# Weight tiles padded to whole multiples of 512 bytes in a one-core decoder block

## The chip, the cores and the metric

The kernel runs on one core of a Trainium2 chip. The metric is the device time of one execution in microseconds. Three executions of the kernel before took 2819.47, 2820.7 and 2825.2 us; the median is 2820.7.

## The reference

One layer of a hybrid decoder block on x (512 tokens, 2048 channels), in float32:

```
mod = silu(c) @ w_ada + b_ada                  # six rows of 2048: shift, scale, gate, twice
h   = rmsnorm(x, norm_mix_g) * (1 + sc_m) + sh_m
a_b, a_c, a_x, q, f_logit, i_in, g_out, gate_a, gate_b = split(h @ w_in)   # 2048 -> 11264
y_a = (a_b * causal_depthwise_conv(a_c * a_x)) @ w_conv_out
y_b = (rmsnorm(hgrn2_chunked(silu(q), 1 - f, i_in, log f)) * silu(g_out)) @ w_hgrn_out
x   = x + gt_m * ((sigmoid(gate_a) * y_a + sigmoid(gate_b) * y_b) @ w_o)
h2  = rmsnorm(x, norm_ffn_g) * (1 + sc_f) + sh_f
x   = x + gt_f * ((silu(h2 @ w_ffn_gate) * (h2 @ w_ffn_up)) @ w_ffn_down)  # 2048 -> 5632 -> 2048
out = rmsnorm(x, norm_final_g)
```

## The kernel before

Activations lie transposed, channels on partitions, 512 tokens along the row. Every large product is made in split precision: weights and activations are each cut into a rounded part (hi) and the remainder (lo), both of type float32r, and each product becomes three matmuls, hi on hi, hi on lo and lo on hi. `mm3` (L228) issues them on L233, L234 and L235 for the projections; `m3` (L628) on L629, L630 and L631 for the gates and the FFN. The weights are the operand that is loaded into the array, 128 x 128 at a time; the activations stream past, 512 or 256 columns of them. `v_block` (L344) is the exception: there the activations are loaded and the weight tile streams, 256 columns at a time.

A weight tile comes in by a DMA on SP's queue as a raw tile (`w_dma`, `g_dma`, `u_dma`), ScalarE casts it to hi, VectorE subtracts hi from it to make lo (L166 and L167 in `w_prep`; `quad_s` at L673 for Strassen quads; L1085 and L1086 in `u_prep` otherwise). The hi and lo tiles are made by `w_tile` (L138) from pools with three buffers of each, `wp` (L84, up to the output projection) and `wp2` (L1050, the FFN), and one of 16 for the tail (`us["pool"]`, L1235). The buffers of a pool come round in the order first, third, second.

The stages, in order of time: the first projections together with the norm and the first adaLN rows; the remaining projections (`proj`, 512 columns streaming) with the HGRN core and the convolution as background work on VectorE, interleaved by step counts; the gates (`st_pass`, 256 columns: one level of Strassen's scheme, seven products on a quad of 128 x 128 blocks); the branch outputs and the output projection, with the other 128 tiles of `w_ada` reduced on VectorE meanwhile (`mods`, L593; two buffers `wm`); the FFN, whose gate and up passes are Strassen passes of 256 columns, and whose `down` (L1159) has 512 columns; the tail, 256 columns.

Where the tiles lie: `w_tile` makes a tile of a*b + 32 elements of 4 bytes and starts the weights at its first element, or, when `half` is set, at the 17th (`WOFF` = 16 elements, 64 bytes). `half` is set for weights past which 256 columns stream. A tile of 1024 weights is 4224 bytes, 8 x 512 + 128; one of 896 is 3712 bytes, 7 x 512 + 128. So consecutive buffers drift by 128 bytes modulo 512. In `wp` the hi buffers start at bytes 117760, 121984 and 126208 of a partition (0, 128 and 256 modulo 512), the lo buffers at 130432, 134656 and 138880 (384, 0 and 128). In `wp2` they start at 39936, 43648 and 47360 (0, 128, 256) and 51072, 54784 and 58496 (384, 0, 128). With the order of the buffers, successive weight tiles have hi/lo at 0/384, 256/128 and 128/0 when 512 columns stream, and at 64/448, 320/192 and 192/64 when 256 do. Activations lie at 0 (`h`, `o`, `sa`, `sx`) or, behind `wp2`, at 256 (`hc`, `sb`). Eight weight pairs of the FFN's first up pass are kept inside `sb` tiles for its second half (kind H of `u_prep`), at 256, with 256 columns streaming.

Of the kernel before, what the change touches and what calls it, by code (L numbers as in the profile page):

```python
# [9 lines left out]
F32R = mybir.dt.float32r  # L10
# [4 lines left out]
P = 128  # L15
# [29 lines left out]
WOFF = 16  # L45
# [17 lines left out]
def hybrid_block_kernel(ctx: ExitStack, tc: tile.TileContext, xt, cols, crow, wam, war, wst, win, wco, who, wo, wgt, wg, wu, wd,  # L63
# [4 lines left out]
    def nm(s):  # L68
        cnt[0] += 1
        return f"{s}{cnt[0]}"  # L70
# [62 lines left out]
        return t.rearrange("p a b -> p (a b)")  # L133

    wlist = []
    wstate = {"dma": 0, "prep": 0, "use": 0, "raw": {}, "hl": {}, "half": ()}

    def w_tile(pool, shape, tag, name, half):  # L138
        a, b = shape[1:]
        t = pool.tile([P, a * b + 32], F32R, tag=tag, name=nm(name))  # L140
        o = WOFF if half else 0
        return t[:, o:o + a * b].rearrange("p (a b) -> p a b", b=b)

    def w_pair(shape, half=False):
        return [w_tile(wp, shape, t, t, half) for t in ("hi", "lo")]
# [824 lines left out]
    torder = [(j, 0) for j in range(TU)] + [(j, 1) for j in range(TU)] + [(j, u) for j in range(TU, 8) for u in range(2)]  # L970
    ulist.extend((wd[j, 10], u, "D" if i < TU else "T") for i, (j, u) in enumerate(torder))
    kept = []
    us = {"dma": 0, "prep": 0, "use": 0, "raw": {}, "hl": {}, "pool": None, "after": ()}

    def u_dma():
        i = us["dma"]
# [86 lines left out]
    def u_prep():  # L1063
        i = us["prep"]
        while i not in us["raw"]:
            u_dma()
        _, u, kind = ulist[i]
        raw = us["raw"].pop(i)[:, u, :, :]
        pool = us["pool"] if kind == "T" else wp2
        shp = [P, 4, P] if kind == "T" else [P, 7, P]  # L1070
        if kind == "H":
            k = len(kept)
            t = sb[k // 2][k % 2]
            hi, lo = (t[:, 1 + 2 * b:3 + 2 * b, :].rearrange("p a (c n) -> p (a c) n", n=P) for b in range(2))
            kept.append((hi, lo))
        else:
            hi = w_tile(pool, shp, "hi", "uh", kind != "D")
            lo = w_tile(pool, shp, "lo", "ul", kind != "D")
        if kind == "S":
            quad_s(wp2.tile([P, 4, P], F32, tag="sm", name=nm("us"), bufs=2), raw, hi, lo)  # L1080
        else:
            with ExitStack() as order:
                for ins in us["after"] if i >= len(ulist) - 12 else ():
                    order.enter_context(tc.issue_after(ins.ins))
                S.copy(hi[:, 0:4, :], raw)  # L1085
                V.tensor_tensor(lo[:, 0:4, :], raw, hi[:, 0:4, :].bitcast(F32), op=ALU.subtract)  # L1086
        us["hl"][i] = (hi, lo)
        us["prep"] = i + 1
# [315 lines left out]
```

## Time and profile before

| | |
|---|---|
| median of three runs | 2820.7 us |
| the profiled execution | 2818.55 us |
| its span, first to last instruction | 2816.8 us |
| TensorE matmul busy | 2741.5 us (97%), 18524 matmuls |
| TensorE weight loads busy | 2461.4 us (87%) |
| VectorE busy | 2217.8 us (79%) |
| ScalarE busy | 1100.1 us (39%) |
| mean granted TensorE clock | 0.991 |

How to read what follows. In a group's line stand the source line, the engine, the operation, the tile written and the tiles read (buffer numbers left out), the shapes, the count, and behind a bar the busy time in us and the mean duration of one instruction in ns, then the idle time before the group. Matmuls are pipelined: one's recorded duration runs on while the next has begun, so durations of successive matmuls overlap. What a matmul costs in a stream is the distance from its start to the next start. In the timeline a row begins with the start and the duration in us. A line of stretches gives its length and the busy time (and count) of TensorE's matmuls, its weight loads, VectorE, ScalarE and GpSimd, then the granted clock, the busy share of the DMA engines and GB/s. The chain is the work that ended last, followed back from the end of the stretch, by engine and line. Residues below are byte addresses modulo 512 within a partition.

### The profile page before, as it was taken

To read this page: it belongs to the slowest core of one execution; us is meant where nothing else is said; L and a number is where in the kernel's file an instruction comes from. 1 tells how busy PE (TensorE), PEld (TensorE's weight loads), DVE (VectorE), ACT (ScalarE), POOL (GpSimd) and SP (SyncE) were. 2 spreads that over 40 slices of the span, in tenths; PEclk is the share of its full clock that TensorE was granted. 3 is DMA by queue.
4 is the path that set the end of the run, shared out by engine and by line. 5 is a ranking of instruction groups with operands and counts; after the bars stand their busy time and mean duration, and the time that the engine had idled before them with its cause. 6 is when DMAs were issued, how large, how long until landed. Compare 5 with 4: busy or idle time off the path is not lost.

```text
span 2816.8 us, 46688 instructions
## 1 busy us (share of the span) xinstructions
PE 2741.5 (97%) x18524; PEld 2461.4 (87%) x18524; DVE 2217.8 (79%) x4326; ACT 1100.1 (39%) x1723; POOL 1.3 (0%) x7
## 2 busy tenths in 40 slices
PE   5999999999999999899999999999999999999997
PEld 3788888888799997787899899998989989898997
DVE  7998963836799996786789787796968879687786
ACT  4333422323245552222375343343434334343445
POOL 0000000000000000000000000000000000000000
PEclk8999999999999999999999999999999999999999
DMA  9865632322233348898744333333333333333333
GB/s 351 302 215 187 207 100 83 97 91 90 76 101 118 124 148 298 294 315 287 239 143 127 100 112 101 109 106 98 113 99 112 99 104 113 98 113 98 105 106 105
DMA packets 117616, 414.23 MB, mean 147 GB/s; under 512 B 12818, under 2 KB 17170, under 8 KB 117396
## 3 DMA queue, kind: packets, MB, share of 16 engines
q1 hardware_dynamic: 116244, 407.04, 43.9%
q10 hardware_dynamic: 1152, 4.19, 0.4%
q8 instruction: 145, 2.38, 0.4%
q14 instruction: 75, 0.61, 0.1%
HBM read 398.59 MB, written 12.59 MB: 146 GB/s over the span
## 4 chain that ended last, share of the span: by engine, by line
PE 81%; DVE 8%; DMA 8%; issue 2%; ACT 1%; SPq 0%; DVEq 0%; ACTq 0%
PE st L631 18%; PE st L630 18%; PE st L629 18%; PE m L233 7%; PE m L235 7%; PE m L234 7%; DMA wm<-in_war_dram 6%; DVE o L311 2%; DVE wm L311 1%; DVE lo L167 1%; PE x L488 1%; PE m L353 1%; PE m L351 1%; PE m L352 1%; PE m L631 1%
## 5 line engine op out<-in xcount | busy, mean ns | idle before, releaser
L233 PE MATMUL m<-h,hi 128*128 128x512 f32 (+1 forms) x1152 | 436.0, 380 | 18.2 <-ACT hi L166 14.8
L631 PE MATMUL st<-sb,ul 128*128 128x256 f32 x1638 | 452.4, 276 | 0.3 <-DVE ul L680 0.3
L630 PE MATMUL st<-sb,uh 128*128 128x256 f32 x1638 | 452.3, 276 | 0.0
L629 PE MATMUL st<-sb,uh 128*128 128x256 f32 x1638 | 452.2, 276 | 0.0
L235 PE MATMUL m<-h,lo 128*128 128x512 f32 (+1 forms) x1152 | 437.0, 379 | 7.9 <-DVE lo L167 7.7
L234 PE MATMUL m<-h,hi 128*128 128x512 f32 (+1 forms) x1152 | 435.1, 378 | 0.3 <-DVE h L338 0.3
L166 ACT CAST hi<-wr 128x1024 fp32r<-128x1024 f32 (+2 forms) x199 | 201.7, 1017 | 532.9 <-PE m L234 381.7
L167 DVE TENSOR_TENSOR lo<-wr,hi 128x1024 fp32r<-128x1024 f32 (+2 forms) x199 | 234.8, 1182 | 118.1 <-ACT hi L166 116.9
L674 ACT CAST uh<-ur 128x384 fp32r<-128x384 f32 x326 | 167.3, 513 | 362.0 <-PE st L630 239.5
L631 PEld LDWEIGHTS st<-sb,ul 128*128 128x128 f32 x1638 | 307.6, 188 | 1.0 <-DVE ul L680 0.5
L629 PEld LDWEIGHTS st<-sb,uh 128*128 128x128 f32 x1638 | 307.5, 188 | 0.4
L630 PEld LDWEIGHTS st<-sb,uh 128*128 128x128 f32 x1638 | 307.5, 188 | 0.0
L233 PEld LDWEIGHTS m<-h,hi 128*128 128x128 f32 x1152 | 219.7, 191 | 62.5 <-ACT hi L166 15.9
L235 PEld LDWEIGHTS m<-h,lo 128*128 128x128 f32 x1152 | 217.6, 189 | 52.8 <-DVE lo L167 13.2
L629 PE MATMUL st<-hc,uh 128*128 128x512 f32 (+1 forms) x656 | 256.9, 392 | 2.9 <-ACT hc L1245 2.0
L631 PE MATMUL st<-hc,ul 128*128 128x512 f32 (+1 forms) x656 | 257.5, 395 | 0.0
L630 PE MATMUL st<-hc,uh 128*128 128x512 f32 x648 | 255.4, 394 | 0.0
L234 PEld LDWEIGHTS m<-h,hi 128*128 128x128 f32 x1152 | 218.0, 189 | 42.7 <-DVE h L338 1.1
L1086 DVE TENSOR_TENSOR ul<-ur,uh 128x512 fp32r<-128x512 f32 x210 | 143.2, 686 | 141.0 <-ACT uh L1085 140.9
L1085 ACT CAST uh<-ur 128x512 fp32r<-128x512 f32 x210 | 129.0, 620 | 314.0 <-PE st L630 294.2
L680 DVE TENSOR_TENSOR ul<-us,uh 128x512 fp32r<-128x512 f32 x326 | 223.0, 684 | 1.7 <-ACT uh L678 1.6
L678 ACT CAST uh<-us 128x512 fp32r<-128x512 f32 x326 | 201.5, 618 | 51.1 <-DVE us L677 50.3
(306 smaller groups left out, 6199.0 us busy)
## 6 DMA issues: line engine op xcount, KB each, us to landing
wm<-in_war_dram SPq DMA_DIRECT2D x128, 512.0 KB, 4.5
wr<-in_win_dram SPq DMA_DIRECT2D x107, 512.0 KB, 3.5
ur<-in_wg_dram SPq DMA_DIRECT2D x96, 512.0 KB, 3.5
ur<-in_wu_dram SPq DMA_DIRECT2D x88, 512.0 KB, 3.5
ur<-in_wd_dram SPq DMA_DIRECT2D x88, 512.0 KB, 3.5
o<-in_wam_dram SPq DMA_DIRECT2D x64, 512.0 KB, 6.5
wr<-in_wgt_dram SPq DMA_DIRECT2D x60, 512.0 KB, 3.6
wr<-in_wo_dram SPq DMA_DIRECT2D x44, 512.0 KB, 4.2
```

The lines of the kernel that those rows point to most:

```text
L166: S.copy(flat(hi)[:, 0:nw], raw[:, 0:nw])
L167: V.tensor_tensor(flat(lo)[:, 0:nw], raw[:, 0:nw], flat(hi)[:, 0:nw].bitcast(F32), op=ALU.subtract)
L233: TE.matmul(ps, wh, ah, start=first, stop=False)
L234: TE.matmul(ps, wh, al, start=False, stop=False)
L235: TE.matmul(ps, wl, ah, start=False, stop=last)
L629: TE.matmul(ps, wh, ah, start=first, stop=False, skip_group_check=True)
L630: TE.matmul(ps, wh, al, start=False, stop=False, skip_group_check=True)
L631: return TE.matmul(ps, wl, ah, start=False, stop=last, skip_group_check=True)
L674: S.copy(hi[:, 0:3, :], raw[:, 1:4, :])
L678: S.copy(hi[:, 3:7, :], sm)
L680: V.tensor_tensor(lo[:, 3:7, :], sm, hi[:, 3:7, :].bitcast(F32), op=ALU.subtract)
L1086: V.tensor_tensor(lo[:, 0:4, :], raw, hi[:, 0:4, :].bitcast(F32), op=ALU.subtract)
```

## The change

`w_tile` makes its tiles larger. Outside the tail a tile has a*b + 16 elements rounded up to a multiple of 128 elements, which is 512 bytes: 4608 bytes for 1024 weights and 4096 for 896. The weights start at the first element or, with `half`, at the 17th, as before. So in `wp` and `wp2` all hi and lo weights with 512 columns lie at 0 modulo 512, and those with 256 columns at 64. In the tail's pool a tile keeps its 32 extra elements. `us` is made earlier, so that `w_tile` can tell the tail's pool. Six buffers grow by 384 bytes each, so whatever is allocated behind `wp` or `wp2` on the same side (`hc`, `sb`, the work tiles `b`, the tail's tiles) moves by 2304 bytes, 256 modulo 512.

```diff
+    us = {"pool": None}
...
     def w_tile(pool, shape, tag, name, half):
         a, b = shape[1:]
-        t = pool.tile([P, a * b + 32], F32R, tag=tag, name=nm(name))
         o = WOFF if half else 0
+        t = pool.tile([P, a * b + 2 * WOFF if pool is us["pool"] else (a * b + WOFF + 127) // 128 * 128], F32R, tag=tag, name=nm(name))
         return t[:, o:o + a * b].rearrange("p (a b) -> p a b", b=b)
...
-    us = {"dma": 0, "prep": 0, "use": 0, "raw": {}, "hl": {}, "pool": None, "after": ()}
+    us.update({"dma": 0, "prep": 0, "use": 0, "raw": {}, "hl": {}, "pool": None, "after": ()})
```

## The prediction

> **What bounds the kernel now.** I read the page's head first, then the chain that ended last, cut into stretches of the span, then the matmul groups, then single weight tiles.
>
> ```profile
> span 2816.8 us, 46688 instructions
> PE 2741.5 (97%) x18524; PEld 2461.4 (87%) x18524; DVE 2217.8 (79%) x4326; ACT 1100.1 (39%) x1723; POOL 1.3 (0%) x7
> ```
>
> TensorE is busy for 97% of the span. But a busy engine isn't everywhere the one that sets the end, so here is the chain cut into stretches. From 0 to 165 us:
>
> ```profile
> by line: DVE o L311 26.6%; DVE lo L167 9.9%; PE m L235 8.4%; PE m L233 7.6%; PE m L234 7.2%; issue 5.8%; DMA x<-in_xt_dram 5.4%; DVE x L335 3.5%; DVE h L338 3.4%; DVE b L360 2.8%; ACT hi L166 2.6%; SPq L291 1.9%; PE m L353 1.6%; ACT b L358
> ```
>
> From 165 to 780 us:
>
> ```profile
> by line: PE m L233 25.8%; PE m L235 25.4%; PE m L234 25.3%; PE x L488 4.9%; PE m L353 4.0%; PE m L352 4.0%; PE m L351 4.0%; PE x L545 1.2%; PE x L555 1.1%; PE x L535 0.9%; PE x L547 0.9%; issue 0.8%; PE x L516 0.7%; PE x L529 0.4%; ACT L743
> ```
>
> From 1063 to 1370 us:
>
> ```profile
> by line: DMA wm<-in_war_dram 53.9%; DVE wm L311 12.4%; issue 10.9%; DMA modrow<-c_scratch 7.7%; DVE lo L167 4.6%; DMA b<-u_scratch 1.7%; DVE o L218 1.6%; DVE x L905 1.5%; DVE b L904 1.5%; DVE x L890 1.1%; DVE x L914 0.9%; SPq L153 0.8%; DVE
> ```
>
> From 1525 to 2755 us:
>
> ```profile
> by line: PE st L631 33.1%; PE st L630 33.1%; PE st L629 33.0%; DMA ur<-in_wu_dram 0.4%; DVE x L914 0.1%; DVE ul L1086 0.1%; DVE us L675 0.1%; DVE hc L1244 0.1%; DVE hc L1251 0.1%; DVE hc L1254 0.0%; ACT e L1250 0.0%; DVE hc L1253 0.0%; DVE
> ```
>
> Stretch two (the projections, 165 to 780) and stretch four (the FFN, 1525 to 2755) are TensorE almost alone: a nanosecond off a matmul there is a nanosecond off the end. Between 1063 and 1370 TensorE isn't in the head of the chain at all: the adaLN rows stream in by DMA, two buffers deep, VectorE reduces each, and that sets the pace. In the first 165 us TensorE has 8.4 + 7.6 + 7.2 = 23% of the chain.
>
> **What the matmuls cost, by where their weights lie.** Each product is a trio: hi weights on the hi activations, the same hi weights on the lo activations, lo weights on the hi activations (L233 to L235, or L629 to L631). One `down` stage shows one turn of its three pairs of weight buffers, four trios each. The starts of the four first matmuls:
>
> ```profile
> 2060.28 0.39 PE L629 MATMUL st<-hc,uh 128*128 128x512 f32 x1
> ...
> 2063.05 0.39 PE L629 MATMUL st<-hc,uh 128*128 128x512 f32 x1
> ...
> 2065.83 0.40 PE L629 MATMUL st<-hc,uh 128*128 128x512 f32 x1
> ...
> 2068.64 0.39 PE L629 MATMUL st<-hc,uh 128*128 128x512 f32 x1
> ```
>
> By the order of the buffers these are the pairs with hi at residue 0 modulo 512 (lo at 384), hi at 256 (lo at 128) and hi at 128 (lo at 0). They take 2.77, 2.78 and 2.81 us: the same twelve matmuls, and the pair at 128 is slower. Twelve trios take 8.36 us, 696.7 ns each. The groups inside each pair say where it sits; the second number behind the bar is the mean duration in ns. The pair at 0:
>
> ```profile
> L630 PE MATMUL st<-hc,uh 128*128 128x512 f32 x4 | 1.6, 396 | 0.0
> L629 PE MATMUL st<-hc,uh 128*128 128x512 f32 x4 | 1.6, 389 | 0.0
> L631 PE MATMUL st<-hc,ul 128*128 128x512 f32 x3 | 1.2, 397 | 0.0
> ```
>
> The first line of the pair at 256, which agrees:
>
> ```profile
> L629 PE MATMUL st<-hc,uh 128*128 128x512 f32 x4 | 1.6, 389 | 0.0
> ```
>
> And of the pair at 128:
>
> ```profile
> L629 PE MATMUL st<-hc,uh 128*128 128x512 f32 x4 | 1.6, 396 | 0.0
> ```
>
> L629's matmul runs while the same hi weights are loaded again for L630 (in the timeline each load starts right behind the start of the matmul before): 389 ns when they lie at 0 or at 256, 396 at 128. The last matmul of each pair runs while the next pair's hi weights are loaded. From lo at 384 to hi at 256 it takes:
>
> ```profile
> L631 PE MATMUL st<-hc,ul 128*128 128x512 f32 x1 | 0.4, 397 | 0.0
> ```
>
> From 128 to 128:
>
> ```profile
> L631 PE MATMUL st<-hc,ul 128*128 128x512 f32 x1 | 0.4, 404 | 0.0
> ```
>
> And from 0 to 0:
>
> ```profile
> L631 PE MATMUL st<-hc,ul 128*128 128x512 f32 x1 | 0.4, 393 | 0.0
> ```
>
> The step from weights at 0 to other weights at 0 is the cheapest of the three, 393. Durations overlap. One turn's sum per trio is (8 x 389 + 4 x 396)/12 = 391.3 for the first line, 396 for the second, (9 x 397 + 397 + 404 + 393)/12 = 397.3 for the third: 1184.6 ns, 487.9 over the 696.7 of the starts, about 163 each.
>
> **The change, part by part.**
>
> *512 columns.* All hi and lo tiles come to 0. The first line takes 389 and the third 393, as the rows show. The second (same activations' other half, then lo weights at 0 behind hi at 0) occurs nowhere before; its ends are 389, the cheapest row, and 404, the dearest step. Like the third it goes to other weights, so I take the third's row, 393. The trio is then 389 + 393 + 393 = 1175, less 487.9, 687 ns: 9.6 saved. Over the whole FFN the first line's mean stands above the turn's 391.3 (the duration is the number in front of the second bar):
>
> ```profile
> L629 PE MATMUL st<-hc,uh 128*128 128x512 f32 x640 | 251.7, 393 | 0.8 <-DVE x L914 0.8
> ```
>
> So 393 - 391.3, nearly 2 ns, comes from something that residue doesn't explain, and I count 8 ns instead of 9.6. That row gives 640 trios. The projections, from 165 to 780 us, have 673:
>
> ```profile
> L235 PE MATMUL m<-h,lo 128*128 128x512 f32 x673 | 267.2, 397 | 0.0
> ```
>
> The first 165 us have 128:
>
> ```profile
> L235 PE MATMUL m<-h,lo 128*128 128x512 f32 x128 | 52.6, 412 | 4.7 <-DVE lo L167 4.4
> ```
>
> And from 1050 to 1375 us there are 256 + 151 = 407:
>
> ```profile
> L235 PE MATMUL m<-o,lo 128*128 128x512 f32 x256 | 102.8, 402 | 4.8 <-DVE lo L167 4.8
> L235 PE MATMUL m<-h,lo 128*128 128x512 f32 x151 | 60.9, 403 | 3.0 <-DVE lo L167 3.0
> ```
>
> TensorE sets the pace in the FFN and the projections. The sum: (640 + 673) x 8 ns = 10.5 us; 128 x 8 x 0.23 = 0.2 us; the 407 count nothing, since the DMA chain covers them (3.3 us if that cover were gone).
>
> Is there a rule against this? The Trainium skill (TensorE: Matmul & The Clock Gate, Part 2, step 1) says that TensorE has two independent SBUF read ports, so that loading the next weights takes no read bandwidth from the running matmul. By that, an address would change nothing and the time would stay at 2820.7. This trace disagrees: 389 against 396 for one line, one shape, one stage.
>
> *256 columns.* They lie at 64, 192, 320 and 448 before, and at 64 after. Starts in the FFN's Strassen passes, 21 matmuls to a weight tile: of a tile with hi at 64, of the next, at 320, and of the one after the tile at 192 that follows:
>
> ```profile
> 1730.27 0.28 PE L629 MATMUL st<-sa,uh 128*128 128x256 f32 x1
> ...
> 1732.64 0.28 PE L629 MATMUL st<-sa,uh 128*128 128x256 f32 x1
> ...
> 1737.40 0.28 PE L629 MATMUL st<-sa,uh 128*128 128x256 f32 x1
> ```
>
> 2.37 us for the one, 4.76 for the other two: 113 ns a matmul wherever the tile lies. I take 0; a hundredth either way in 2.38 is 0.5 ns a matmul, and over the FFN's (1,631 + 656) x 3 matmuls, in the first two rows below, at most 3 us either way.
>
> ```profile
> L631 PE MATMUL st<-sb,ul 128*128 128x256 f32 x1631 | 450.3, 276 | 0.0
> ...
> L631 PE MATMUL st<-sa,ul 128*128 128x256 f32 x656 | 181.2, 276 | 0.0
> ```
>
> Rows of the whole run, and of the projections' `v_block`, at other places:
>
> ```profile
> L629 PE MATMUL m<-sb,sb 128*128 128x256 f32 x30 | 8.5, 283 | 0.0
> ...
> L353 PE MATMUL m<-lo,h 128*128 128x256 f32 x208 | 58.6, 282 | 1.6 <-DVE lo L167 1.6
> ```
>
> The kept weights inside the `sb` tiles lie at 256 and, as everything behind the smaller pool moves by 2,304 bytes, come to 0: 283 ns against 276 at 64. At 512 columns 0 and 256 both read 389, so nothing changes here. In `v_block` the weight tile streams and the activations (at 0 already) are loaded; its third line, 282 x208, is 6 ns from 276, so at most 208 x 3 x 6 ns = 3.7 us if all of it were due to residue; either sign is open, and I take 0.2 us gained.
>
> *What moves with it.* `hc` and `sb` shift from 256 to 0; activations of the projections lie at 0 already and their L235 row shows 397 like the FFN's 397. No instruction, wait or DMA is added or removed; the tiles' writers keep their shapes. Behind the saved time, what is late next in the two TensorE stretches is VectorE: its busy time has to stay under theirs.
>
> ```profile
> 165.00:780.00 615.00, 611.56 (x3801) 506.79 (x3799) 424.74 (x581) 197.97 (x206) 0.00 (x0) 1.00 0.38 121
> ```
>
> The other two stretches:
>
> ```profile
> 1063.00:1370.00 307.00, 293.39 (x1279) 236.35 (x1277) 223.57 (x295) 73.28 (x74) 0.00 (x0) 0.98 0.86 297
> 1525.00:2755.00 1230.00, 1228.46 (x8805) 1144.01 (x8803) 988.62 (x2241) 497.80 (x895) 0.00 (x0) 1.00 0.33 105
> ```
>
> VectorE (third pair) is busy 425 of 615 and 989 of 1230 us; 5 us less leaves room. From 1063 to 1370 the DMA share of 0.86 is why I grant nothing.
>
> Sum: 10.5 + 0.2 + 0.2 = 10.9 us. The profiled execution took 2818.55 (span 2816.8 and 1.75 around it), 2.2 under the median of 2820.7; taken from it 2807.7, from the median 2809.8.
>
> **Rivals.**
>
> *The gain is kept in one stretch only* (chance 0.06). The projections carry VectorE's background work in program order; if that became the pace there, as it is from 0 to 165 us, only the FFN's 640 x 8 = 5.1 us would remain: 2815.6, within 0.2% of no change. Against it: 425 of 615 us busy, and TensorE's lines head the chain.
>
> *Residue isn't the cause* (0.04): the pair at 128 is slow for another reason, say its place in the turn, and moving it changes nothing: 2820.7. Against it: the two steps between equal residues differ (404 and 393), and 389 comes back at both 0 and 256. This is also the rival that the Trainium skill's rule above (TensorE: Matmul & The Clock Gate, Part 2, step 1) stands for.
>
> *Equal residues collide* (0.04, slower). At 128 the step to other weights at the same residue is the dearest, 404. If hi and lo at 0 behave like that in the second line and, with all tiles equal, in the third, a trio is 389 + 404 + 404 = 1197, less 487.9, 709 ns, 12.4 more: 1313 x 12.4 = 16.3, so 2837.0. It makes the kernel slower from the point where the second and third line together pass 796 ns (1184.6 - 389); two steps of 393 are 786. Against it: the one row for 0 to 0 is 393, not 404.
>
> **How the numbers follow.** The forecast has 0.86. Its own range: with the second line at 389, 9.6 + 4 = 13.6 ns a trio, 17.9 us, 2802.8, and about 2 us more if 256 columns gain: 2801. With the second line left at 396 and the unexplained 1.6 ns taken off, 5 ns, 6.6 us: 2814.1. To hold the time 8 times in 10 I go up to 2817, over the half-gain rival. A measurement of this kernel tells about 0.2% (5.6 us) from nothing. The forecast is faster through all its range: 0.86; the first two rivals are no change: 0.10; the third is slower: 0.04.
>
> **What would show it.** Right: in the changed profile L629 and L233 at 512 columns near 389 to 391 throughout, L630/L631 and L234/L235 near 393, 12-matmul tiles of `down` all 2.75 us, the two TensorE stretches shorter by some 5 us each, 256 columns still 276, and the stretch from 1063 to 1370 as long as before with more waiting of TensorE on L167. Wrong: any 512-column line at 396 or above, 276 rising, or new waits in the projections.

## The result and the profile after

The changed kernel is slower: 2837.18 us median of seven runs (2831.37 to 2851.39) against 2820.73 of seven runs before (2817.11 to 2828.8). The ratio is 1.0062, with a 95% interval of 1.0039 to 1.0086. The forecast was 2809.8, faster. The profiled execution took 2844.18 us, so its trace shows a larger loss (25.6 us by the two profiled times) than the medians do. The line numbers after are one higher than before: L233 is now L234, L629 is L630.

The page after, its head and the groups of Strassen matmuls and weight loads (columns as before: busy us, mean ns of one, idle):

```profile
span 2842.4 us, 46688 instructions
...
PE 2760.2 (97%) x18524; PEld 2497.8 (88%) x18524; DVE 2231.6 (79%) x4326; ACT 1094.1 (38%) x1723; POOL 1.3 (0%) x7
...
L632 PE MATMUL st<-sb,ul 128*128 128x256 f32 x1638 | 460.0, 281 | 0.1
L631 PE MATMUL st<-sb,uh 128*128 128x256 f32 x1638 | 459.9, 281 | 0.0
L630 PE MATMUL st<-sb,uh 128*128 128x256 f32 x1638 | 459.9, 281 | 0.0
...
L630 PEld LDWEIGHTS st<-sb,uh 128*128 128x128 f32 x1638 | 314.0, 192 | 0.4
L632 PEld LDWEIGHTS st<-sb,ul 128*128 128x128 f32 x1638 | 307.5, 188 | 0.7 <-DVE ul L681 0.3
L631 PEld LDWEIGHTS st<-sb,uh 128*128 128x128 f32 x1638 | 307.6, 188 | 0.0
```

The 256-column matmuls went from 276 to 281 ns, and one weight load of three from 188 to 192. Before, that load's row read:

```profile
L629 PEld LDWEIGHTS st<-sb,uh 128*128 128x128 f32 x1638 | 307.5, 188 | 0.4
```

The groups with 512 columns of the FFN after, from 1525 to 2755 us:

```profile
L630 PE MATMUL st<-hc,uh 128*128 128x512 f32 x640 | 250.6, 392 | 1.0 <-DVE x L915 1.0
L631 PE MATMUL st<-hc,uh 128*128 128x512 f32 x640 | 249.4, 390 | 0.0
L632 PE MATMUL st<-hc,ul 128*128 128x512 f32 x640 | 247.5, 389 | 0.0
```

These gained, and more than forecast: 393, 396 and 397 before. Take every matmul's distance from its start to the next in both traces, and count one that holds a wait like the mean of the others of its kind. Then the 5,568 with 512 columns sum to 1291.8 us before and 1266.1 after (-25.7), the 10,980 with 256 columns in `mm3` and `m3` to 1247.3 and 1289.2 (+41.9), the 768 of `v_block` to 90.8 and 92.0 (+1.2). What waits add to these groups goes from 77 to 85 us.

Cut at the first matmuls of the gates, of the branch outputs, of the output projection's half tiles and of the FFN's Strassen passes, and at the last 512-column matmul of `down`, the parts of the span changed by -4.0, +9.8, -1.3, +2.3, +16.6 and +2.2 us. The gates, which have no 512-column matmul, show the loss without a gain beside it: 290.6 us before, 300.4 after. These two stretches are the first lines of two answers, before and after; behind the length stand TensorE, its loads, VectorE and ScalarE:

```profile
780.90:1071.50 290.60, 290.60 (x2551) 290.60 (x2552) 269.46 (x652) 145.29 (x266) 0.00 (x0) 0.99 0.41 131
```

```profile
776.90:1077.30 300.40, 300.39 (x2550) 300.40 (x2551) 273.25 (x652) 145.81 (x267) 0.00 (x0) 1.00 0.40 127
```

TensorE is busy all through both: the same 2,550 matmuls take longer each. Their starts are 113.3 ns apart before and 117.8 after (in the FFN 113.4 and 117.8). Only the beginning of the stretch before is different: some 14 matmuls there are 213 ns apart, at a granted clock of 0.50. They cost that stretch some 1.5 us, so by their pace the gates lost some 11 us:

```profile
781.00:784.00 3.00, 3.00 (x14) 3.00 (x15) 0.86 (x2) 0.35 (x1) 0.00 (x0) 0.50 0.02 7
```

The changed kernel's gates begin at a clock of 1.00; the last experiment comes back to that.

The longer pace is not everywhere. From 1530 to 1564 us of the changed kernel, with the weights at 64 as in the rest of the FFN, the groups read:

```profile
L631 PE MATMUL st<-sb,uh 128*128 128x256 f32 x69 | 19.0, 276 | 0.0
L632 PE MATMUL st<-sb,ul 128*128 128x256 f32 x69 | 19.0, 276 | 0.0
L630 PE MATMUL st<-sb,uh 128*128 128x256 f32 x68 | 18.8, 276 | 0.0
```

The same lines, shapes and addresses modulo 512 run at 276 here and at 281 behind the next `down`. An address that has a fixed price can't do that. It looks like two cadences of one stream, that is, two steady paces, 113 and 118 ns, and the question is what sets and what ends the longer one.

### The profile page after: what moved, and what is told of

Read it like the earlier page. It is cut to its first block, busy times and chain, and to the rows that moved or that the text cites. A ratio compares the mean times of both kernels' runs of the same rounds, so it can differ in the third digit from the quotient of the medians.

```text
span 2842.4 us, 46688 instructions
## 1 busy us (share of the span) xinstructions
PE 2760.2 (97%) x18524; PEld 2497.8 (88%) x18524; DVE 2231.6 (79%) x4326; ACT 1094.1 (38%) x1723; POOL 1.3 (0%) x7
## 4 chain that ended last, share of the span: by engine, by line
PE 80%; DMA 8%; DVE 8%; issue 2%; ACT 1%; SPq 0%; DVEq 0%; ACTq 0%
PE st L630 18%; PE st L631 18%; PE st L632 18%; DMA wm<-in_war_dram 7%; PE m L234 6%; PE m L236 6%; PE m L235 6%; DVE o L312 2%; DVE wm L312 1%; DVE lo L168 1%; PE x L489 1%; PE m L632 1%; PE m L354 1%; PE m L630 1%; PE m L631 1%
## 5 line engine op out<-in xcount | busy, mean ns | idle before, releaser
L632 PE MATMUL st<-sb,ul 128*128 128x256 f32 x1638 | 460.0, 281 | 0.1
L631 PE MATMUL st<-sb,uh 128*128 128x256 f32 x1638 | 459.9, 281 | 0.0
L630 PE MATMUL st<-sb,uh 128*128 128x256 f32 x1638 | 459.9, 281 | 0.0
L234 PE MATMUL m<-h,hi 128*128 128x512 f32 (+1 forms) x1152 | 434.7, 379 | 16.9 <-ACT hi L167 13.9
L630 PEld LDWEIGHTS st<-sb,uh 128*128 128x128 f32 x1638 | 314.0, 192 | 0.4
L632 PEld LDWEIGHTS st<-sb,ul 128*128 128x128 f32 x1638 | 307.5, 188 | 0.7 <-DVE ul L681 0.3
L631 PEld LDWEIGHTS st<-sb,uh 128*128 128x128 f32 x1638 | 307.6, 188 | 0.0
L234 PEld LDWEIGHTS m<-h,hi 128*128 128x128 f32 x1152 | 217.4, 189 | 56.5 <-ACT hi L167 15.0
L630 PE MATMUL st<-hc,uh 128*128 128x512 f32 (+1 forms) x656 | 255.7, 390 | 3.0 <-ACT hc L1246 2.0
L632 PE MATMUL st<-hc,ul 128*128 128x512 f32 (+1 forms) x656 | 252.6, 388 | 0.0
```

The costliest lines, as they stand in the source:

```text
L234: TE.matmul(ps, wh, ah, start=first, stop=False)
L630: TE.matmul(ps, wh, ah, start=first, stop=False, skip_group_check=True)
L631: TE.matmul(ps, wh, al, start=False, stop=False, skip_group_check=True)
L632: return TE.matmul(ps, wl, ah, start=False, stop=last, skip_group_check=True)
```

## The experiments

Theory A: the longer cadence keeps itself up while hi and lo come from one residue; a different residue ends it. Its rivals: B, that the drift from tile to tile ended it before; C, that residue 64, or the shift of `hc` and `sb`, costs 4 ns as such; and a fixed price of equal residues. In all experiments below, the arithmetic is the kernel's own.

**Lo at 192, hi at 64.**

```diff
-        o = WOFF if half else 0
+        o = (WOFF + 32 * (tag == "lo" and pool is not us["pool"])) if half else 0
```

> The changed kernel, but where 256 columns stream the lo weights start at 192 modulo 512 instead of 64; hi stays at 64 in every tile, 512 columns stay at 0. In the changed kernel's trace the 512-column matmuls start 227 ns apart (232 before) and the 256-column ones 117.7 ns (113.4 before). Theory A: a stream of 256-column matmuls has two cadences, 113 and 118 ns, and the slow one keeps itself up only while every load comes from the same residue, so hi and lo at different residues end it: 256 columns at 113.4, the 512-column gain remains, about 16 us under the kernel before, near 2804. Theory B: what ended the slow cadence in the kernel before was the drift from one weight tile to the next; there is none here: 256 columns at 117.7, near 2837. Theory C: 64 as such, or hc and sb having moved to 0, costs the 4 ns: near 2837 as well.

Measured: 2805.23 us, ratio 0.9946 (0.9928 to 0.9965). The FFN's groups, 1525 to 2755 us:

```profile
L632 PE MATMUL st<-sb,ul 128*128 128x256 f32 x1626 | 449.1, 276 | 0.0
L630 PE MATMUL st<-sb,uh 128*128 128x256 f32 x1625 | 448.7, 276 | 0.0
L631 PE MATMUL st<-sb,uh 128*128 128x256 f32 x1625 | 448.7, 276 | 0.0
...
L631 PE MATMUL st<-hc,uh 128*128 128x512 f32 x640 | 249.4, 390 | 0.0
L632 PE MATMUL st<-hc,ul 128*128 128x512 f32 x640 | 247.6, 389 | 0.0
```

Moving lo by 128 bytes, with no drift between tiles and `hc` and `sb` where the change put them, brings 276 back and keeps the gain at 512 columns. B and C don't stand as put.

**The kernel before, with hi and lo equal.** (Besides the lines shown, `us` is made earlier, as in the change.)

```diff
+        tail = pool is us.get("pool")
-        t = pool.tile([P, a * b + 32], F32R, tag=tag, name=nm(name))
-        o = WOFF if half else 0
+        t = pool.tile([P, a * b + (32 if tail else 160)], F32R, tag=tag, name=nm(name))
+        o = (WOFF + 32 * (tag == "lo" and not tail)) if half else 0
```

> The kernel before, but where 256 columns stream hi and lo of a tile lie at the same residue: 64, then 320, then 192 from tile to tile. 512 columns as before, hc and sb at 256 as before. Theory A (equal residues of hi and lo keep the slow cadence up): 256 columns near 117.7 ns, about 40 us over the kernel before, 2860. If one change of residue from tile to tile, every 21 matmuls, is enough to end it (theory B): 113.4 ns and 2821. Theory C (64 as such, or the moved hc and sb): 2821.

Measured: 2822.66 us, ratio 1.0004 (0.9994 to 1.0015): no loss. Theory A as first put missed by some 37 us. The trace says why: behind a `down` whose 512-column weights still drift, the stream enters the 113 ns cadence in all ten stretches and stays there, so there was nothing to end. At the gates it did begin at 118 ns, and held for 20 trios through the steps from 64 to 320 and on to 192, before it fell to 113 at the step to 64.

**Each part of the change alone.**

512 columns undone (drifting again), 256 columns at 64:

```diff
-        o = WOFF if half else 0
+        o = WOFF
+        if not half:
+            k = turn[id(pool), tag] = turn.get((id(pool), tag), -1) + 1
+            o = {"hi": (0, 64, 32), "lo": (96, 32, 0)}[tag][k % 3]
```

> The changed kernel with the part for 512 columns undone: hi/lo of these weights lie at 0/384, 256/128 and 128/0 again, 256 columns stay at 64/64, tiles and all other addresses as in the changed kernel. Theories A, B and C agree that the 256-column part alone is a loss of some 40 us: 512 columns at 232 ns, 256 columns at 117.7, near 2860. If the two parts act on each other (the 512-column stages set off the slow cadence), it would be well under 2850.

Measured: 2829.4 us, ratio 1.0033 (1.0016 to 1.005), far from 2860. Two of its passes, 1615 to 1680 us and 1736 to 1800 us (lines are five higher than before):

```profile
L634 PE MATMUL st<-sb,uh 128*128 128x256 f32 x138 | 38.1, 276 | 0.0
...
L634 PE MATMUL st<-sb,uh 128*128 128x256 f32 x130 | 36.5, 281 | 0.0
```

Hi and lo at 64 throughout, yet one stretch is at 276 and the next at 281, each from end to end: 2 of the 10 stretches behind a `down` are long ones, and in the changed kernel all 10. So the parts do act on each other: 512 columns at 0 hand over to 256 columns in the longer cadence. A long stretch of 658 matmuls costs 2.9 us (658 x 4.4 ns), so two of them are 5.8 of the 6.3 us by which the median here is longer. The twelve runs spread over 26 us, those of the experiment before over 9; that would fit an entry that differs from run to run, which the one trace can't show.

256 columns undone (64/448, 320/192, 192/64 again), 512 columns at 0:

```diff
-        o = WOFF if half else 0
+        o = 0
+        if half:
+            o = WOFF
+            if pool is not us["pool"]:
+                k = turn[id(pool), tag] = turn.get((id(pool), tag), -1) + 1
+                o = {"hi": (16, 80, 48), "lo": (112, 48, 16)}[tag][k % 3]
```

> The changed kernel with the part for 256 columns undone: hi/lo of these weights at 64/448, 320/192 and 192/64 again, 512 columns at 0/0, tiles and all other addresses as in the changed kernel, hc and sb at 0. Theories A and B: 256 columns at 113.4 ns, 512 columns at 227, near 2804. Theory C, as far as it blames hc and sb at 0: 117.7 ns and near 2837.

Measured: 2804.27 us, ratio 0.9941 (0.9923 to 0.9959). The part for 512 columns is worth 0.6% by itself, and `hc` and `sb` at 0 cost nothing that shows; this version and the one with lo at 192 beat both kernels.

**A few tiles only.**

```diff
-        o = WOFF if half else 0
+        o = (WOFF + 32 * (half == 2 and tag == "lo")) if half else 0
...
-        hi, lo = w_pair((P, 8, P), True)
+        hi, lo = w_pair((P, 8, P), 2 if i == 1 else True)
...
+            half = kind != "D"
+            if kind in "SC":
+                n = sum(x[2] in "SCH" for x in ulist[:i]) % 8
+                if n in (1, 2) and ulist[i - n - 1][2] == "D":
+                    half = 2
```

> The changed kernel, with lo at 192 in 21 of the weight tiles past which 256 columns stream: the second tile of the gates, and the second and third tile of each FFN pass behind a down stage. All other such tiles keep hi and lo at 64. Theory A (two cadences, each keeping itself up; a different residue ends the slow one, and nothing then brings it back until TensorE next waits or goes through 512 columns): the 21 tiles (147 of some 3,470 trios) put nearly the whole gates and FFN at 113.4 ns, near 2806. A fixed price of equal residues, paid by each matmul that has them: 147 of 3,470 trios are 4% of the 42 us, under 2 us, near 2835.

Measured: 2807.69 us, ratio 0.9947 (0.9935 to 0.996). 4% of the trios undid nearly the whole loss. The timeline (start, duration in us) of the second tile behind a `down`, whose lo weights at 192 come first with L632 at 1608.57:

```profile
1608.09 0.28 PE L631 MATMUL st<-sb,uh 128*128 128x256 f32 x1
1608.21 0.28 PE L632 MATMUL st<-sb,ul 128*128 128x256 f32 x1
1608.33 0.28 PE L630 MATMUL st<-sa,uh 128*128 128x256 f32 x1
1608.45 0.28 PE L631 MATMUL st<-sa,uh 128*128 128x256 f32 x1
1608.57 0.28 PE L632 MATMUL st<-sa,ul 128*128 128x256 f32 x1
1608.68 0.28 PE L630 MATMUL st<-sa,uh 128*128 128x256 f32 x1
1608.80 0.28 PE L631 MATMUL st<-sa,uh 128*128 128x256 f32 x1
1608.91 0.28 PE L632 MATMUL st<-sa,ul 128*128 128x256 f32 x1
1609.03 0.28 PE L630 MATMUL st<-sb,uh 128*128 128x256 f32 x1
1609.14 0.28 PE L631 MATMUL st<-sb,uh 128*128 128x256 f32 x1
```

Four starts up to 1608.57 are 0.12 apart, from 1608.68 on they are 0.11 to 0.12, 0.46 us in four where it had been 0.48. From 1612 to 1680 us, where almost all tiles are at 64/64 again, the groups read 276; from 1525 to 1560, where no tile was altered, 281, though those tiles read 276 in the changed kernel (1530 to 1564 us above):

```profile
L630 PE MATMUL st<-sb,uh 128*128 128x256 f32 x144 | 39.7, 276 | 0.0
...
L630 PE MATMUL st<-sb,uh 128*128 128x256 f32 x68 | 19.1, 281 | 0.0
```

Behind a `down` all 10 stretches begin long and turn short at the altered tiles, where in the changed kernel all 10 stay long. So the cadence is a state of the stream that outlives what set it. A fixed price of 64 and 64 is ruled out. The gates, some 11 us of the loss, are no evidence here: in this trace they begin at a granted clock of 0.51 (778.3 to 781.6 us), and behind such a beginning they run short in the last experiment too, where all weights lie at 192.

**Lo at 320.** The edit is the first one with 64 in place of 32.

> As the run with lo at 192, but with lo at 320: 256 bytes from hi instead of 128. If what counts is that the loads come from different residues modulo 512, 256 columns start every 113.4 ns and the time is near 2805. If it is the residue modulo 256 (512-column loads at 0 and at 256 read the same 389 ns before), hi and lo count as equal and the time is near 2837.

Measured: 2840.33 us, ratio 1.0057 (1.0043 to 1.0071), and 281 in the FFN's groups:

```profile
L630 PE MATMUL st<-sb,uh 128*128 128x256 f32 x1590 | 446.4, 281 | 0.0
L631 PE MATMUL st<-sb,uh 128*128 128x256 f32 x1590 | 446.4, 281 | 0.0
L632 PE MATMUL st<-sb,ul 128*128 128x256 f32 x1589 | 446.3, 281 | 0.3 <-DVE ul L681 0.3
```

256 bytes apart count as equal. 128 bytes apart (lo at 192) do not.

**The changed kernel once more.**

> The changed kernel unaltered, profiled once more. With a fixed price per address each stage comes out as in its first profile, every 256-column matmul at 117.7 ns between 777 and 1385 us and behind every down stage. With two cadences whole stretches between waits may come out at 113 ns this time, with no address changed, and the span may differ by several us from 2842.4.

Measured: one run, 2840.0 us, span 2838.2. The long stages were the same: 10 of 10 behind `down`, and the gates. So the entry behind `down` is regular while 512 columns lie at 0. But one shorter stretch flipped, the end of the output projection's half tiles, which begins behind a wait of TensorE. In the first profile (1438.5 to 1453 us) and in this one (1435 to 1450 us) it reads:

```profile
L234 PE MATMUL m<-h,hi 128*128 128x256 f32 x43 | 11.9, 276 | 0.0
...
L234 PE MATMUL m<-h,hi 128*128 128x256 f32 x43 | 12.1, 281 | 0.0
```

One program, the same addresses, two paces: the expectation was borne out there, on the scale of 15 us and not of a stage.

**Equal in each tile, drifting between tiles, 512 columns at 0.** This tells A from B with an entry that is known to be long.

```diff
         o = WOFF if half else 0
+        if half and pool is not us["pool"]:
+            k = turn[id(pool), tag] = turn.get((id(pool), tag), -1) + 1
+            o = (16, 80, 48)[k % 3]
```

> The changed kernel, where 256 columns stream hi and lo at the same residue in each tile, but 64, 320 and 192 from tile to tile; 512 columns at 0 as in the changed kernel, so that every stretch of 256 columns begins in the slow cadence. Theory A as first put (equal residues of hi and lo keep it up): slow throughout, 117.7 ns, near 2837. Theory A': any two successive loads that differ by 128 modulo 256 disturb it, those of two tiles too: the step from 64 to 320 leaves it slow, 320 to 192 and 192 to 64 end it, so that it lasts a few tiles (7 trios each) after each of some 20 entries and never returns: near 2808.

Measured: 2804.62 us, ratio 0.994 (0.9916 to 0.9964). One pass, from 1600 to 1605 us and from 1606 to 1670 us:

```profile
L634 PE MATMUL st<-sb,uh 128*128 128x256 f32 x11 | 3.1, 281 | 0.0
...
L634 PE MATMUL st<-sb,uh 128*128 128x256 f32 x135 | 37.3, 276 | 0.0
```

A pass begins long, holds for 9, 16 or 23 trios (a remainder of 2 and then one, two or three tiles of 7) and stays short for the rest. A as first put, which asks for hi and lo to differ, does not fit. Theory A' has the time right and one of its steps wrong. By the turn of the offsets, the long cadence ended at a step from 192 to 64 in all ten passes and at the gates. The step from 320 to 192, equally 128 modulo 256, ended it nowhere: in the passes the trio there takes some 358 ns in place of 353, and the next is at 353 again. Nor did a step from 192 to 64 only two trios behind a `down`, which is why some passes hold for 23.

**Both at 192.** The edit is the first one without its condition on the tag.

> The changed kernel with hi and lo both at 192 instead of both at 64 where 256 columns stream. If equal residues keep the slow cadence up, whichever they are, 256 columns start 117.7 ns apart and the time is near 2838. If 64 itself is the costly address, 113.4 ns and near 2805.

Measured: 2847.79 us, ratio 1.0094 (1.0067 to 1.0122). So 64 isn't special. But the gates of its profiled execution, with all weights at 192, ran at 276 nearly from their start, and the FFN's groups show 279 to 280, with starts 117.8 ns apart behind every `down`:

```profile
L630 PE MATMUL st<-h,hi 128*128 128x256 f32 x425 | 117.3, 276 | 0.0
...
L630 PE MATMUL st<-sb,uh 128*128 128x256 f32 x1597 | 445.6, 279 | 0.0
```

These gates began long and then had some 16 matmuls 213 ns apart, at a granted clock of 0.51, after which the stream was in the short cadence; equal residues didn't take it out of it:

```profile
777.20:780.50 3.30, 3.30 (x18) 3.30 (x17) 0.20 (x2) 0.73 (x2) 0.00 (x0) 0.51 0.00 0
```

That holds over all eleven traces. In six (before, lo at 192, each part alone, a few tiles, both at 192) the gates begin with such matmuls and run at 113 ns within a few trios of the clock's return. In the other five they begin at 118. So whether the gates were long in a trace went with the clock at their start, and not with the addresses alone; that the clock is what sets it was not tested. The four runs of this experiment fit: two took 2842.3 and 2842.4 us, the latter the profiled one with short gates, and two 2853.2 and 2853.4, 11 us more, which is what the gates cost in the long cadence (2,550 x 4.4 ns).

## Why the prediction was wrong, point by point

*256 columns* is the step that failed: "113 ns a matmul wherever the tile lies. I take 0", with at most 3 us either way. It was +41.9 us over the run's 10,980 such matmuls, and "276 rising", one of its own signs of being wrong, came true. Every tile in the rows for that step had hi and lo 128 bytes apart modulo 256 (64/448, 320/192, 192/64). They showed that the tile's place has no price; they could not show what equal places do, since only the change made them equal. A warning stood in the prediction's own rows: the kept weights, 283 ns, have hi and lo at one residue (256), and `v_block`, 282, loads activations whose hi and lo lie at one residue (0). I read the 283 as the price of 256 and 0. Taken as a bound for equal residues, 7 ns on 276, it would have given up to 66 us for the 9,411 matmuls of the FFN's Strassen rows and the gates (2,287 x 3 + 2,550), and a range that reaches to slower. The true cost was 4.4 ns a matmul in the long stretches.

As a price the 283 would have misled, since the kept weights run at a third pace: their starts are 120 ns apart and all three loads of a trio take 192 ns, from the first kept weight on, without a wait. In the changed kernel they also do what 512 columns at 0 do. The rows below are of loads at 64/64 ahead of them (1465.7 to 1467.4 us), of the kept weights behind their last wait (1476 to 1480), and of loads at 64/64 behind them (1481 to 1491):

```profile
L630 PE MATMUL m<-sa,uh 128*128 128x256 f32 x6 | 1.7, 276 | 0.0
...
L630 PE MATMUL m<-sa,sb 128*128 128x256 f32 x12 | 3.4, 283 | 0.0
...
L630 PE MATMUL m<-sa,uh 128*128 128x256 f32 x29 | 8.1, 281 | 0.0
```

*`v_block`* was taken at 0.2 us gained, with the sign open and at most 3.7 us. Its pace went from 118.2 to 119.9 ns, 1.2 us lost; in the projections it lost 3.9 us, most of it in waits.

*512 columns* was right in direction and too small. The second line, for which there was no row, came out at 390, next to the bound of 389, and the third at 389 instead of 393. 4.6 ns a matmul, 13.9 a trio, make 18.2 us for the 1,313 trios where 10.5 were forecast. The run with 256 columns as before confirms it: its ratio of 0.9941 is a gain of 17 us (12 to 22 by the interval).

*The stretch from 1063 to 1370 us* was right: its part of the span changed by 1.3 us although its matmuls gained. After, the chain there still reads

```profile
by line: DMA wm<-in_war_dram 61.2%; issue 11.1%; DVE wm L312 11.1%; DMA modrow<-c_scratch 4.0%; DVE lo L168 3.3%; DVE o L219 1.5%; DMA gc<-o_scratch 1.4%; DVE x L906 0.8%; DVE h L219 0.7%; DVE b L905 0.7%; PE m L236 0.7%; PE m L235 0.5%; PE
```

and TensorE's waits for lo took up most of the gain there. In the prediction's rows from 1050 to 1375 us they are 4.8 + 3.0 = 7.8 us; after, 5.1 + 6.3 = 11.4:

```profile
L236 PE MATMUL m<-o,lo 128*128 128x512 f32 x256 | 101.0, 395 | 5.1 <-DVE lo L168 5.1
...
L236 PE MATMUL m<-h,lo 128*128 128x512 f32 x145 | 57.6, 397 | 6.5 <-DVE lo L168 6.3
```

*The projections* with everything ahead of them gave 4.0 us, where 5.4 were forecast for their 673 trios. Their 512-column matmuls gained 9.1 us, waits included. `v_block` took back 3.9 of it, and the part ahead of them, where VectorE heads the chain, grew by 1.3. As the FFN's 512-column matmuls gained 9.2 us, the rival of a gain in one stretch only is out. *The rival of colliding equal residues* had the sign and the kind of cause right and the place wrong: it put the collision at 512 columns, where equality helped, and its 2837.0 agrees with the median only by chance. *Residue isn't the cause* is out: moving lo by 128 bytes moves the time by 32 us.

*The ports.* The rule of the Trainium skill (TensorE: Matmul & The Clock Gate, Part 2, step 1), that loading weights takes no read bandwidth from the running matmul, doesn't account for these runs: the placing of the loaded weights changed the pace of both shapes, 232 to 227 ns and 113 to 118.

What stays open is why loads at equal residues modulo 256 leave a stream of 256 columns in its longer cadence, why 512 columns at 0 hand over to it, and why the step from 192 to 64 ends it where the one from 320 to 192 doesn't. The traces show the weight loads of that cadence (192 instead of 188 ns in one of three) but not what they contend for.

## What to carry to other kernels

A pace measured on rotating buffers holds for that rotation: before all buffers are made alike, look for a row in which they are alike already. A matmul stream can have two steady paces for the same instructions, so a stretch that is uniformly a few per cent dearer may be a matter of how it was entered; look at the pace stretch by stretch, not at the mean. Of the placings tried here the best have the weights with 512 columns at 0 and, where 256 stream, some steps of 128 bytes: 2805.23 us with lo at 192, 2804.27 with the old drift, 2804.62 with hi and lo drifting together. These three do not differ beyond the spread of their runs.

## What the runs showed of the hardware

Matmuls with 256 columns, a fresh weight load each and all loads at 64 modulo 512 ran at either 113 or 118 ns from start to start. In the run with 512 columns drifting, one stretch was at the one pace and the next at the other; in two profiles of the changed kernel, the same stretch was.

The longer pace ended at a load at 64 behind one at 192: in the run with a few tiles the first lo tile at 192 was used at 1608.57 us, and from 1608.68 on the starts are 113 to 114 ns apart. A step of 256 bytes (lo at 320) didn't end it. It also ended without any change of address: after some 16 matmuls at a granted clock of 0.51 (both at 192), after waits, and in the changed kernel behind a single trio of 382 ns (at 1511.76 us; 353 ahead of it, 340 from the third trio behind it). Streams with all loads at 64 were in it behind waits, behind 512 columns (all 10 times with these at 0, 2 of 10 with these drifting) and behind the kept weights at 0.

The kept weights, with all loads at 256 before and at 0 after, ran 256 columns at a third pace, 120 ns, with all three loads of a trio at 192 ns.

With 512 columns, loads that all start at 0 gave 227 ns a matmul, against 232 on average where they stepped between 0, 128, 256 and 384.
